# Neighbourhood attention: both heads' scores in one two-bank PSUM tile

## The chip, the cores and the metric

The kernel runs on one core of a Trainium2 chip. The metric is the device time of one execution in microseconds (us). Before the change the median of three runs is 2096.86 us (2092.8 to 2097.57).

## The reference, cut to what matters

The model has two layers over 512 latent tokens (a grid of 8 rows by 64 columns) and 256 context tokens. Each layer has one input projection whose columns go to three groups of heads: latent attention ("mla"), neighbourhood attention ("na") and a gated DeltaNet ("dn", a scan over chunks). The change is in the neighbourhood attention, which has 4 heads of width 64:

```
scale = NA_D ** -0.5
s_loc = einsum(qg, kb) * scale + bias        # each query: 8 rows x 16 columns around it
s_loc = where(col_ok, s_loc, -inf)
s_ctx = einsum(qg, ck) * scale               # and all 256 context keys
p = softmax(concatenate([s_loc, s_ctx], -1))
o = einsum(p_loc, vb) + einsum(p_ctx, cv)
```

In the first layer the 256 context tokens are queries too and read only context keys; in the second layer they are not.

## The kernel before, in words

Four heads are two pairs. The two heads of a pair lie in the two halves of the partitions (0 to 63 and 64 to 127), so that a product of one head uses 64 rows of TensorE. `attention()` goes over the pairs and, inside a pair, over blocks of 128 queries: six blocks in the first layer (four of latent tokens, two of context tokens), four in the second. That makes 12 blocks and 8 blocks.

For one block (lines 853 to 917 of the profile's numbering):

- The scores `s_na`. Each operand is held as a high and a low part, and three products (`nkh` with `nqh`, `nkl` with `nqh`, `nkh` with `nql`) are summed. A block of latent queries takes them over 256 local keys and again over 256 context keys: 12 products, 6 for each head. A block of context queries has 6, 3 for each head. The loops at 868 and 871 name the heads in turn, head 1 and then head 0.
- The softmax, head by head. VectorE (DVE) takes the maximum over the context scores (L877), adds the bias to the local scores and takes their maximum (L881), and makes the negated maximum (L883). ScalarE (ACT) takes the exponentials of the local part (L884) and, straight from PSUM, of the context part (L885): that is the last read of the scores. DVE then makes and applies the reciprocal (L889 to L891).
- TensorE transposes the weights (`tp_na`, L896), ACT copies one head's and DVE the other's to `pt` (L898), TensorE multiplies with the values (`o_na`), and ACT takes the result away (L909).

Before the change each head's scores are a PSUM tile of one bank, taken by `att_bank("s_na")` from a tag "S" with two buffers; the transposes and `o_na` share three more banks under the tag "T". A tile's buffer is free for the next block once all reads of the tile are done.

The order of the instructions on each engine isn't that of the source. A scheduler reorders the whole program when it is built, by its own reckoning of when operands and buffers are free, and each engine then runs its list strictly in order. `beside()` mixes steps of the DeltaNet scan (`ks`, `qs`, `yp`, `sp`, `oa`, and the chunk inverses `pp`, `yq`) and, in the first layer, columns of the modulation product (`acc_ada`, `tr_ada`) with the attention blocks. In the second layer, blocks of attention also stand between the last input projections (`acc_in`), by the string `TAIL`. After neighbourhood attention comes latent attention (`s_mla`, `tp_mla`, `o_mla`), mixed with the output projection `acc_o`.

All matrix products are issued by the helper at L104, so the profile tells them apart by tile name.

Of the kernel before, what the change touches and what calls it, by code (L numbers as in the profile page):

```python
# [9 lines left out]
F32 = mybir.dt.float32  # L10
# [7 lines left out]
P = 128  # L18
# [84 lines left out]
def mm(nc, out, lhsT, rhs, start=True, stop=True):  # L103
    nc.tensor.matmul(out, lhsT, rhs, start=start, stop=stop)  # L104
# [258 lines left out]
def layer(tc, nc, a, l, es_x, xT, env, nx):  # L363
    e = env
    V, S, G, PE = nc.vector, nc.scalar, nc.gpsimd, nc.tensor
# [467 lines left out]
    psA = pool(es_a, f"psA{l}", 1, PSUM, "left")  # L833
    att_n = BN

    def att_bank(name):
        tag = "S" if name[:2] == "s_" else "T"
        return psA.tile([P, 512], F32, tag=tag, name=name, bufs=att_n[tag])
# [8 lines left out]
    def attention():  # L847
        for pair in range(2):
# [4 lines left out]
            for qt in range(nT // P):  # L853
                is_ctx = qt >= 4
                tok = slice(qt * P, (qt + 1) * P)
                c0 = (0, 8, 24, 32, 0, 0)[qt]
                var = (0, 1, 1, 2, 0, 0)[qt]
                vb = ((0, 1), (6, 7), (7, 8), (2, 3), (), ())[qt] + (4, 5)
                lo_ = 256 if is_ctx else 0
                pts, ss = [], [att_bank("s_na") for j in range(2)]  # L860
                hs = [slice(64 * j, 64 * j + 64) for j in range(2)]
                cutk = lambda t, j: grid(t)[hs[j], :, c0:c0 + 32].rearrange("p r (b c) -> p b r c", b=2)


                trio = ((qh, kh), (qh, kl), (ql, kh))
                if not is_ctx:
                    for i, (q_, k_) in enumerate(trio):
                        for j in (1, 0):
                            mm(nc, ss[j][:, 0:256], q_[hs[j], tok], cutk(k_, j), i == 0, i == 2)
                for i, (q_, k_) in enumerate(trio):  # L870
                    for j in (1, 0):
                        mm(nc, ss[j][:, 256:512], q_[hs[j], tok], k_[hs[j], CTX], i == 0, i == 2)
                for j in range(2):
                    s_ = ss[j]
                    st_ = sn.tile([P, 8], F32, tag="st", name="st", bufs=4)
                    pr = sn.tile([P, 512], F32, tag="pr", name="pr", bufs=2)
                    V.reduce_max(out=st_[:, 0:1], in_=s_[:, 256:512], axis=AX.X)  # L877
                    if is_ctx:
                        V.tensor_scalar(out=st_[:, 2:3], in0=st_[:, 0:1], scalar1=-1.0, scalar2=None, op0=ALU.mult)
                    else:  # L880
                        V.tensor_tensor_reduce(out=pr[:, 0:256], in0=s_[:, 0:256], in1=gm[:, j, var].rearrange("p b r c -> p (b r c)"),  # L881
                                               scale=1.0, scalar=NEG, op0=ALU.add, op1=ALU.max, accum_out=st_[:, 1:2])
                        V.tensor_scalar(out=st_[:, 2:3], in0=st_[:, 0:1], scalar1=st_[:, 1:2], scalar2=-1.0, op0=ALU.max, op1=ALU.mult)  # L883
                        S.activation(out=pr[:, 0:256], in_=pr[:, 0:256], func=AF.Exp, bias=st_[:, 2:3], accum_out=st_[:, 3:4])  # L884
                    S.activation(out=pr[:, 256:512], in_=s_[:, 256:512], func=AF.Exp, bias=st_[:, 2:3], accum_out=st_[:, 4:5])  # L885
                    if is_ctx:
                        V.reciprocal(out=st_[:, 5:6], in_=st_[:, 4:5])
                    else:
                        tt(out=st_[:, 6:7], in0=st_[:, 3:4], in1=st_[:, 4:5], op=ALU.add)  # L889
                        V.reciprocal(out=st_[:, 5:6], in_=st_[:, 6:7])  # L890
                    V.tensor_scalar(out=pr[:, lo_:512], in0=pr[:, lo_:512], scalar1=st_[:, 5:6], scalar2=None, op0=ALU.mult)  # L891
                    tp = att_bank("tp_na")
                    nb = 2 if is_ctx else 4
                    for b in range(nb):
                        o2 = lo_ + b * P
                        PE.transpose(tp[:, b * P:(b + 1) * P], pr[:, o2:o2 + P], ident)  # L896
                    pt = sn.tile([P, 512], F32, tag="pt", name="pt", bufs=3)
                    (S.copy if j == 0 else V.tensor_copy)(out=pt[:, 0:nb * P], in_=tp[:, 0:nb * P])  # L898
                    pts.append(pt)
                o_ = att_bank("o_na")  # L900
                for b in range(len(vb)):
                    for j in (1, 0):
                        hd = 2 * pair + j
                        mm(nc, o_[j * 64:j * 64 + 64, 0:P], nav[:, vb[b], hd * 64:hd * 64 + 64], pts[j][:, b * P:(b + 1) * P],
                           b == 0, b == len(vb) - 1)
                if is_ctx:
                    S.copy(out=o_na[:, tok], in_=o_[:, 0:P])
                else:
                    S.copy(out=grid(o_na)[:, :, 16 * qt:16 * qt + 16], in_=o_[:, 0:P].rearrange("p (r c) -> p r c", c=16))  # L909
                if qt == nT // P - 1:  # L910
                    nc.sync.dma_start(out=d_o[2 + pair][:, 0:nT], in_=o_na[:, 0:nT])
                    if l == 0 and e.dbg is not None and "na" in e.dbg:
                        nc.sync.dma_start(out=e.dbg["na"][:, pair], in_=o_na)
                yield True

    na = attention()

    bm = C("bm32").rearrange("p (b c) -> p b c", b=4)
# [210 lines left out]
    psA, att_n, ada = pool(es_a, f"psM{l}", 1, PSUM, "left"), BM, iter(ADA[1])  # L1129
# [33 lines left out]
    for pair in range(2):  # L1163
# [30 lines left out]
        for qt in range(nT // P):  # L1194
# [5 lines left out]
            pts = []  # L1200
            for j in range(2):
# [4 lines left out]
                ss = []  # L1206
# [273 lines left out]
```

## Time and profile before

| | |
|---|---|
| median of the runs | 2096.86 us |
| the profiled execution | 2095.13 us, of which the span of instructions 2093.4 us |
| TensorE (PE) busy | 1939.7 us, 93% of the span |
| VectorE (DVE) busy | 1177.3 us, 56% |
| ScalarE (ACT) busy | 714.2 us, 34% |
| GpSimd (POOL) busy | 761.6 us, 36% |
| DMA | 232.55 MB, mean 111 GB/s |
| granted TensorE clock | 0.967 of full speed |

The span is dominated by the large products of the feed-forward part and the projections. Neighbourhood attention's scores run at 252 us (the first block, between the projections), from 353 to 450 us (the other eleven blocks of the first layer), and from 1412 to 1534 us (the eight blocks of the second layer). A share over the whole span says little about these stretches; the rows below are of the stretches.

### The profile page before, as it was taken

The numbers are of one execution on the slowest core, as the hardware profiler recorded it, in microseconds if no ns is written. First come the engines' busy times: TensorE is split into PE (matmuls) and PEld (weight loads), VectorE is DVE, ScalarE is ACT, GpSimd is POOL, SyncE is SP. The second block draws the span as 40 slices with busy tenths as digits, with TensorE's granted clock in tenths as the row PEclk, the third lists the DMA queues.
The fourth block names the chain that finished last, engine by engine and source line by source line (L and its number), as shares of the span: only waits on it lengthen the run. The fifth ranks groups of instructions, "written<-read, shape, count | busy, mean of one in ns | idle before, by whom it ended". The sixth has DMA issues, their size and how long they took to land. (4 is left out here: it accounts for less than half of the span.)

```text
span 2093.4 us, 32000 instructions
## 1 busy us (share of the span) xinstructions
PE 1939.7 (93%) x12746; PEld 1644.8 (79%) x12746; DVE 1177.3 (56%) x2045; ACT 714.2 (34%) x1385; POOL 761.6 (36%) x540
## 2 busy tenths in 40 slices
PE   6899998997998999999999988878998889999998
PEld 4778787876877888888888876767787678888887
DVE  4888914877467447256353358984678653213123
ACT  5343233334444121121122344233544443222234
POOL 3466133223323223222322443823322343444444
PEclk9999999998999999999999999999999899999999
DMA  7324253561212335245342431334332232333323
GB/s 283 84 74 140 97 165 110 187 197 59 91 59 85 127 121 161 89 126 156 103 131 76 130 79 61 114 124 129 100 98 70 78 96 71 101 91 95 103 92 93
DMA packets 119308, 232.55 MB, mean 111 GB/s; under 512 B 30516, under 2 KB 55988, under 8 KB 119032
## 3 DMA queue, kind: packets, MB, share of 16 engines
q1 hardware_dynamic: 119160, 230.51, 35.4%
q8 instruction: 100, 1.64, 0.3%
q14 instruction: 48, 0.39, 0.1%
HBM read 199.46 MB, written 31.01 MB: 110 GB/s over the span
## 5 line engine op out<-in xcount | busy, mean ns | idle before, releaser
L217 POOL TENSOR_TENSOR wl<-wr,wh 128x1024 fp32r<-128x1024 f32 (+2 forms) x188 | 440.6, 2344 | 846.1 <-ACT wh L216 826.4
L216 ACT CAST wh<-wr 128x1024 fp32r<-128x1024 f32 (+2 forms) x190 | 193.5, 1019 | 707.9 <-PE acc_gu L104 288.8
L104 PE MATMUL acc_gu<-fh,wh 128*128 128x512 f32 (+1 forms) x1024 | 358.5, 353 | 9.6 <-ACT fh L304 8.8
L104 PE MATMUL acc_gu<-fl,wh 128*128 128x512 f32 (+1 forms) x1024 | 359.8, 352 | 4.1 <-DVE fl L305 4.1
L104 PE MATMUL acc_gu<-fh,wl 128*128 128x512 f32 (+1 forms) x1024 | 358.8, 351 | 0.0
L104 PE MATMUL acc_in<-hh,wh 128*128 128x512 f32 (+1 forms) x640 | 228.3, 360 | 20.4 <-ACT xp L491 8.5
L104 PE MATMUL acc_in<-hl,wh 128*128 128x512 f32 (+1 forms) x640 | 227.7, 357 | 3.0 <-DVE hl L305 2.0
L1361 DVE TENSOR_TENSOR av<-acc_gu,av 128x768 f32<-128x768 f32 (+1 forms) x44 | 36.3, 824 | 337.8 <-PE acc_gu L104 330.9
L104 PE MATMUL acc_in<-hh,wl 128*128 128x512 f32 (+1 forms) x640 | 224.2, 355 | 2.0 <-POOL wl L217 2.0
L104 PEld LDWEIGHTS acc_gu<-fh,wh 128*128 128x128 f32 x1024 | 193.6, 190 | 37.3 <-ACT fh L304 11.0
L104 PEld LDWEIGHTS acc_gu<-fl,wh 128*128 128x128 f32 x1024 | 194.3, 190 | 30.4 <-DVE fl L305 4.3
L104 PEld LDWEIGHTS acc_gu<-fh,wl 128*128 128x128 f32 x1024 | 194.0, 190 | 26.1
L104 PEld LDWEIGHTS acc_in<-hh,wh 128*128 128x128 f32 x640 | 124.3, 195 | 46.1 <-ACT xp L491 10.2
L104 PE MATMUL acc_d<-al,wh 128*128 128x512 f32 (+1 forms) x444 | 157.2, 354 | 0.0
L104 PE MATMUL acc_d<-ah,wh 128*128 128x512 f32 (+1 forms) x444 | 157.2, 354 | 0.0
L104 PE MATMUL acc_d<-ah,wl 128*128 128x512 f32 (+1 forms) x444 | 156.1, 354 | 0.0
L254 DVE CUSTOM_DVE_ANT_0 junk<-wada,scb 128x1024 f32<-128x1024 f32 x112 | 146.2, 1305 | 5.9 <-DMA wada<-w_adaT 3.2
L104 PEld LDWEIGHTS acc_in<-hl,wh 128*128 128x128 f32 x640 | 125.2, 196 | 24.8 <-DVE hl L305 4.5
L104 PEld LDWEIGHTS acc_in<-hh,wl 128*128 128x128 f32 x640 | 124.1, 195 | 20.6 <-issue 3.1
L501 DVE SCALAR_TENSOR_TENSOR cy<-xp,cw,cy 128x770 f32<-128x770 f32 (+1 forms) x96 | 121.4, 1265 | 22.5 <-ACT cy L499 19.0
L1379 DVE SCALAR_TENSOR_TENSOR xT<-acc_d,mod,xT 128x512 f32<-128x512 f32 (+1 forms) x76 | 46.4, 634 | 155.3 <-PE acc_d L104 155.3
L1365 DVE TENSOR_TENSOR al<-av,ah 128x768 fp32r<-128x768 f32 (+1 forms) x44 | 100.4, 2282 | 35.2 <-ACT ah L1364 35.2
(390 smaller groups left out, 3777.2 us busy)
## 6 DMA issues: line engine op xcount, KB each, us to landing
wr<-w_gu SPq DMA_DIRECT2D x88, 512.0 KB, 3.5
wada<-w_adaT SPq DMA_DIRECT2D x56, 512.0 KB, 3.3
wr<-w_in SPq DMA_DIRECT2D x48, 512.0 KB, 3.5
wr<-w_dn SPq DMA_DIRECT2D x32, 448.0 KB, 3.3
wada<-w_ada SPq DMA_DIRECT2D x24, 512.0 KB, 3.5
wada<-w_ada SPq DMA_DIRECT2D x8, 1024.0 KB, 8.1
wr<-w_dn SPq DMA_DIRECT2D x16, 512.0 KB, 3.5
xT<-xT SPq DMA_DIRECT2D x16, 384.0 KB, 4.9
```

Of the source, the lines that this page charges most:

```text
L104: nc.tensor.matmul(out, lhsT, rhs, start=start, stop=stop)
L216: S.copy(out=hi[:, sl], in_=raw[:, sl])
L217: eng.tensor_tensor(out=lo[:, sl], in0=raw[:, sl], in1=hi[:, sl].bitcast(F32), op=ALU.subtract)
L254: V.tensor_tensor_reduce(out=junk, in0=w, in1=scb[:, s], scale=1.0, scalar=0.0, op0=ALU.mult, op1=ALU.add, accum_out=mod[l][:, part, j, s: ...
L501: stt(out=y[:, :wid], in0=xp[:, j:j + wid], scalar=w_(j), in1=y[:, :wid], op0=ALU.mult, op1=ALU.add)
L1361: tt(out=av[:, :nT], in0=accs[1][:, :nT], in1=av[:, :nT], op=ALU.mult)
L1365: after.append(tt(out=l_[:, :nT], in0=av[:, :nT], in1=h_[:, :nT].bitcast(F32), op=ALU.subtract))
L1379: stt(out=xT[:, m, st_], in0=acc, scalar=mod[l][:, 5, m, s:s + 1], in1=xT[:, m, st_], op0=ALU.mult, op1=ALU.add)
```

## The change

```diff
@@ -857,7 +857,8 @@
                 var = (0, 1, 1, 2, 0, 0)[qt]
                 vb = ((0, 1), (6, 7), (7, 8), (2, 3), (), ())[qt] + (4, 5)
                 lo_ = 256 if is_ctx else 0
-                pts, ss = [], [att_bank("s_na") for j in range(2)]
+                pts, s2 = [], psA.tile([P, 2, 512], F32, tag="S", name="s_na", bufs=1)
+                ss = [s2[:, j] for j in range(2)]
                 hs = [slice(64 * j, 64 * j + 64) for j in range(2)]
                 cutk = lambda t, j: grid(t)[hs[j], :, c0:c0 + 32].rearrange("p r (b c) -> p b r c", b=2)
```

The two heads' scores are now the two halves of one tile of two banks, with one buffer. The same two banks are used, each head still has its own, and no instruction is added or removed. What changes is that a block gets both banks at once, when all reads of the block before it are done. Lines after 860 have a number one higher in the changed kernel.

On TensorE, in the first layer, the second and third block's scores stood like this before (`s_na` scores, `ks` and `oa` products of the scan, `pp` of an inverse, `acc_ada` and `tr_ada` of the modulation):

```order
L104 MATMUL oa<-w,At 128x128 x4
L104 MATMUL pp<-p_3901,strips 32x32 x2
L104 MATMUL tr_ada<-cst,adarow 128x2
L104 MATMUL acc_ada<-wada,sc 32x128 x8
L104 MATMUL s_na<-nkh,nqh 128x256
L104 MATMUL s_na<-nkl,nqh 128x256
L104 MATMUL s_na<-nkh,nql 128x256
...
L104 MATMUL ks<-S_3168,dn_k 128x128 x4
L104 MATMUL pp<-p_3901,strips 32x32 x2
```

And in the changed kernel:

```order
L104 MATMUL o_na<-pt,nav 64x128 x8
L104 MATMUL acc_ada<-wada,sc 32x128 x8
L104 MATMUL ks<-S_3168,dn_k 128x128 x3
L104 MATMUL s_na<-nkh,nqh 128x256 x2
L104 MATMUL s_na<-nkl,nqh 128x256 x2
L104 MATMUL s_na<-nkh,nql 128x256 x2
...
L104 MATMUL ks<-S_3168,dn_k 128x128
L104 MATMUL qs<-S_3168,dn_q 128x128
L104 MATMUL tr_ada<-cst,adarow 128x2
```

Before, a stretch holds six products of one head, and the other head's six stand elsewhere; now "x2" is one product of each head, and the twelve stand together. All blocks of the changed kernel have this form.

On TensorE in the second layer, the second block stood between the projections of a weight tile before:

```order
L104 MATMUL acc_in<-hh_10575,wh 128x512
L104 MATMUL acc_in<-hl_10583,wh 128x512
L104 MATMUL s_na<-nkh,nqh 128x256
L104 MATMUL s_na<-nkl,nqh 128x256
L104 MATMUL s_na<-nkh,nql 128x256
...
L104 MATMUL acc_in<-hh_10575,wl 128x512
L104 MATMUL acc_in<-hh_10576,wh 128x512
```

In the changed kernel its first two products stand some 80 instructions further on, and the other ten some 170, behind the chunk inverse (`yq`) and the sum of squares for the latent queries (`ms_q`):

```order
L104 MATMUL yq<-strips,p_13093 32x32 x31
L104 MATMUL ms_q<-cst,sqs 128x2 x4
L104 MATMUL acc_in<-hh_10570,wh 128x512
L104 MATMUL acc_in<-hl_10578,wh 128x512
L104 MATMUL acc_in<-hh_10570,wl 128x512
L104 MATMUL s_na<-nkl,nqh 128x256 x2
L104 MATMUL s_na<-nkh,nql 128x256 x2
...
L104 MATMUL acc_in<-hh_10563,wh 128x512
```

The block has moved back in the row, so that more of other work stands between the first block's softmax and it.

On DVE in the first layer, the two heads' maxima of a block stood together before:

```order
L236 TENSOR_TENSOR mod_88<-tr_ada,bada 128x2
L231 COPY adarow<-acc_ada 128x128
L877 TENSOR_REDUCE st<-s_na 128x1 x2
L1055 TENSOR_TENSOR S_3591<-sp,S_3591 128x512
L1070 TENSOR_TENSOR o_3594<-oa,o_3594 128x512
L236 TENSOR_TENSOR mod_88<-tr_ada,bada 128x2
L881 ISA pr,st<-s_na,gmask_456 128x256
```

In the changed kernel one head's whole start goes first, and steps of the scan (`w`, `dn_q`) stand ahead of the other's:

```order
L878 TENSOR_REDUCE st<-s_na 128x1
L236 TENSOR_TENSOR mod_88<-tr_ada,bada 128x2
L882 ISA pr,st<-s_na,gmask_456 128x256
L882 ISA st 128x1
L899 COPY pt<-tp_na 128x512
L884 TENSOR_SCALAR st<-st 128x1
L1045 TENSOR_TENSOR w<-yp,scal 128x512
L1100 SCALAR_TENSOR_TENSOR dn_q<-o_tp,sml,z 128x4x128
L890 TENSOR_TENSOR st<-st 128x1
L878 TENSOR_REDUCE st<-s_na 128x1
```

Besides, the order of latent attention and of the output projection behind each neighbourhood attention is shuffled a little (in the first layer to about 560 us, in the second to about 1704 us); everything else is in the same order as before.

## Rows read from the trace of the kernel before

**Rows 1.** Windows: busy us of each engine, instructions, granted clock, DMA

```profile
core 0: us, PE busy (x) PEld busy (x) DVE busy (x) ACT busy (x) POOL busy (x), PEclk, DMA share, GB/s
350.00:450.00 100.00, 99.89 (x1386) 86.31 (x1386) 76.04 (x247) 36.28 (x129) 15.21 (x22) 0.98 0.56 172
450.00:560.00 110.00, 90.76 (x650) 76.15 (x650) 74.23 (x162) 50.66 (x147) 33.45 (x35) 0.91 0.34 110
1444.00:1453.00 9.00, 4.47 (x19) 3.08 (x18) 5.05 (x10) 7.30 (x14) 4.20 (x4) 0.80 0.93 211
1486.00:1536.00 50.00, 44.67 (x621) 37.50 (x620) 38.64 (x109) 21.51 (x66) 16.57 (x14) 0.90 0.36 112
1536.00:1640.00 104.00, 86.63 (x764) 74.14 (x759) 79.04 (x164) 47.12 (x143) 31.49 (x38) 0.95 0.25 73
```

**Rows 2.** Waits of PE from 343 to 455 us: total us, times, longest

```profile
PE tr_ada L104 <- DVE adarow L231: 1.6, 1, 1.6
PE sp L104 <- DVE w L1044: 1.0, 1, 1.0
```

**Rows 3.** Timeline of PE: start us, us, operation; one head alone

```profile
363.23 0.38 PE L104 MATMUL s_na<-nkh,nqh 64*128 64x256 f32 x1
363.45 0.28 PE L104 MATMUL s_na<-nkl,nqh 64*128 64x256 f32 x1
363.57 0.28 PE L104 MATMUL s_na<-nkh,nql 64*128 64x256 f32 x1
...
364.13 1.16 PE L104 MATMUL ks<-S,dn_k 128*128 128x128 f32 x8
...
380.71 0.38 PE L104 MATMUL s_na<-nkh,nqh 64*128 64x256 f32 x1
...
381.25 1.16 PE L104 MATMUL yp<-rr,Y 128*128 128x128 f32 x8
```

**Rows 4.** Timeline of PE: the first block, heads in turn

```profile
252.03 0.39 PE L104 MATMUL s_na<-nkh,nqh 64*128 64x256 f32 x2
252.25 0.28 PE L104 MATMUL s_na<-nkl,nqh 64*128 64x256 f32 x2
...
252.73 0.28 PE L104 MATMUL s_na<-nkh,nql 64*128 64x256 f32 x2
252.94 0.39 PE L104 MATMUL acc_v<-wh,hh 128*128 128x256 f32 x1
```

**Rows 5.** Windows of the tile s_na alone, columns of Rows 1 without POOL

```profile
235.00:300.00 65.00, 0.98 (x12) 0.78 (x12) 0.00 (x0) 0.00 (x0) 0.97 0.45 128
345.00:550.00 205.00, 17.74 (x108) 13.44 (x108) 14.05 (x36) 13.01 (x48) 0.94 0.46 145
1340.00:1550.00 210.00, 12.90 (x96) 9.98 (x96) 12.27 (x32) 8.79 (x32) 0.93 0.38 116
```

**Rows 6.** Timeline of PE, second layer: the second block

```profile
1447.96 0.39 PE L104 MATMUL s_na<-nkh,nqh 64*128 64x256 f32 x1 [0.22 <-ACT pr L885]
...
1450.82 0.58 PE L104 MATMUL s_na<-nkh,nqh 64*128 64x256 f32 x1 [1.87 <-ACT pr L885]
```

**Rows 7.** Waits of PE from 1486 to 1536 us

```profile
PE tp_na L896 <- DVE pr L891: 2.7, 2, 1.4
PE o_na L104 <- DVE pt L898: 1.5, 1, 1.5
PE s_na L104 <- ACT pr L885: 0.6, 2, 0.4
```

**Rows 8.** Timeline of DVE: one block's softmax begins, first layer

```profile
364.24 0.76 DVE L877 TENSOR_REDUCE st<-s_na 128x1 f32<-128x256 f32 x2 [0.58 <-PE s_na L104]
```

**Rows 9.** Timeline of ACT: the same block's last read of the scores

```profile
370.93 0.46 ACT L885 ACTIVATE pr<-s_na,st 128x256 f32<-128x256 f32 x1
```

**Rows 10.** Waits of PE from 455 to 560 us, the longest

```profile
PE yp L104 <- DVE rr L1039: 5.9, 2, 4.9
```

## The prediction

> **What bounds the kernel now.** I first asked the windows view for the stretches in which the scores run, since shares over the whole span mix them with the big products. In the first layer, from 350 to 450 us, PE is busy 99.9 of 100 us and DVE 76 [rows 1]. The list of PE's waits over this stretch has two entries, 2.6 us together, and the scores are in neither [rows 2]. So PE sets the pace there, and a microsecond of PE work taken away is a microsecond, as long as DVE keeps up. In the second layer, from 1486 to 1536 us, PE is busy 44.7 of 50 us and DVE 38.6 [rows 1], and PE's waits are for DVE (`pr`, `pt`) and, with 0.6 us, for the exponentials that free the scores' bank [rows 7]. There PE and DVE share the bound. Behind both stretches comes latent attention, where PE is idle for 19 of 110 us and 17 of 104 us, by 90.76 and 86.63 us busy [rows 1], in the first layer mostly on the scan's `rr` from DVE [rows 10].
>
> **What a pair costs, alone and in turn.** The timeline shows a stretch of six products of one head from 363.23 us to the next work at 364.13: 0.90 us; products follow each other every 0.12 us, and the stretch pays about 0.2 us for its first step and its last [rows 3]. A stretch of three (a context block's head) takes from 380.71 to 381.25: 0.54 us [rows 3]. The first block, in which both heads' products happen to alternate, takes from 252.03 to 252.94: 0.91 us for twelve [rows 4]. So two products that use different halves of the rows run beside each other, and a block whose heads go in turn costs what one head costs alone.
>
> **The sum.** Nothing is removed or added; 216 products are put in another order. Of the tile's busy time in the first layer, 17.74 us for 108 products [rows 5], a part overlaps the next work: the six of rows 3 would end 0.28 us after their last start, the twelve of rows 4 are busy 0.98 us [rows 5] but hold PE for 0.91. Taking 0.07 us off each of the 21 stretches that the timeline has there leaves 16.3 us. Afterwards the eleven blocks cost 7 x 0.91 + 4 x 0.54 = 8.5 us, the context blocks' 0.54 being an estimate (three pairs at 0.12 and the 0.2 of a stretch). That takes 7.8 us off PE. In the second layer 12.90 us of busy time [rows 5] in 12 stretches is 12.1 us by the same step; afterwards eight blocks at 0.91 us, and 0.2 us each for two that the new order still cuts in two, are 7.7 us: 4.4 us less. It is less than in the first layer because several blocks there go in turn already. Third, one block of the second layer stands too early before: PE is idle for 1.87 us, until 1450.82, for an exponential of the block before [rows 6]. The new order puts this block behind other work, so that the wait has a reason to go. Together 14.1 us at most.
>
> What of it arrives? In the first layer the stretch is PE's own, and DVE's 76 us of work fit in the 92 that would be left. But the scan's DVE steps are then crowded, and the wait for `rr` of up to 4.9 us behind the stretch [rows 10] has less work ahead of it; for that I take 1.5 us off: 6.3 us arrive. In the second layer half of PE's idle time is set by DVE already [rows 7], so I take half of 4.4 us, 2.2. Of the 1.87 us, half: the projections beside it stood still for a weight as well (PE is busy 4.5 of the 9 us around, DMA at 93% [rows 1]), and what is freed may be waited for there. 6.3 + 2.2 + 0.9 = 9.4 us. From the profiled execution's 2095.13 us that leads to 2085.7; the median of the runs is 1.7 us higher, so 2087.4, rounded to 2087.5.
>
> **What the change adds.** One wait: a block's first product now waits until both heads of the block before have had their exponentials, where it waited for one. Behind it on PE stand steps of the scan and the transposes `tp_na` of the block before, which in turn feed DVE and ACT. The trace has no tile of two banks, so I bound this from both sides. At the good end it costs nothing: in the block of rows 8 and 9 DVE begins at 364.24 us and the last exponential ends at about 371.4, 7.2 us, and that with the scan's work in between; eleven blocks in 100 us are one per 9 us, and the new order puts scores roughly a period apart. At the bad end each of the 18 blocks that follow another in their layer waits as the block of rows 6 did, 1.87 us: 34 us. The rows from 343 to 455 us have no such wait at all [rows 2], those from 1486 to 1536 two, with 0.6 us [rows 7]; I take zero for the first layer, and the halving above covers the second.
>
> **Rivals.**
>
> *DVE takes over.* Both heads' scores are now ready in the same moment, while DVE works on one head after the other, in the new order with steps of the scan before the second. If DVE's latency rather than PE sets the period, PE's 7.8 and 4.4 us turn into waits of `tp_na` and `o_na` for DVE, and the time stays at 2094 to 2100 us. For it: the waits of rows 7, and DVE at 77% in both stretches [rows 1]. Against it: in the first layer PE waits for DVE only 2.6 us in 112 [rows 2]. The Trainium skill, page "TensorEngine Tiling (Array Packing)", section "PSUM Bottleneck", speaks for this rival: it says that packing the array speeds TensorE but not the emptying of PSUM, which may then become the bottleneck. In the trace the second layer agrees in part (2.7 + 1.5 us of waits for DVE in 50 us), the first doesn't. I give it 0.21.
>
> *The pair's wait becomes the period.* One tile, one buffer: if scores, both softmaxes and the release take longer than PE's work for a block, every block waits. Break-even is at 12 us over 18 blocks, 0.67 us a block; from 1.0 us on the kernel is slower by more than can be told from nothing. At 1.87 us a block [rows 6] it is 34 - 12 = 22 us slower, some 2119. For it: the 7.2 us from the first maximum to the last exponential [rows 8, 9], plus 0.9 for the scores, is close to a period of 8.4 us (92 us for eleven blocks). Against it: those 7.2 us contain waiting in DVE's queue, and the row's own steps are 0.76 us for both maxima and 0.46 for an exponential. I give it 0.11.
>
> *The shuffled order behind it is better too.* The stretches of latent attention are reordered as well, and hold 19 and 17 us of idle PE [rows 1]. If a quarter of it goes, and the 14.1 us arrive nearly whole, the time is some 2076 to 2080. The same shuffle could as well cost as much, which would fall in the first rival's place. 0.18.
>
> *The heads' products don't run beside each other after all* I leave without a chance of its own: rows 4 show it done.
>
> **How the numbers follow.** A difference of under 0.3% (6.3 us) can't be told from none here; faster is thus below 2090.6. The forecast (2082 to 2093) has 0.50, of which 0.43 lie below 2090.6; the better order has 0.18, DVE's rival 0.21, the pair's wait 0.11. Faster 0.43 + 0.18 = 0.61, the same 0.07 + 0.21 = 0.28, slower 0.11. The range leaves out the pair's wait and the better order's lower half: 2077 to 2100; the forecast's own is 2082 to 2093.
>
> **What would show it.** In the profile after: every block's scores in one stretch of 0.91 us (0.54 for context blocks), the tile's busy time down from 0.98 + 17.74 + 12.90 = 31.6 us [rows 5] to about 18 (16 blocks at 0.98 us and four at 0.6); the eleven blocks done by about 442 us instead of 450; the wait of 1.87 us gone. Against me would be waits of `s_na` for `pr` (L886 then) of about a microsecond in each block, which is the pair's wait, or longer waits of `tp_na` and `o_na` for `pr` and `pt`, which is DVE's rival. If the stretches shrink as said and the end doesn't come earlier, the gain went into latent attention's waits for DVE.

## The result and the profile after

The changed kernel takes 2077.15 us (median of 4 runs, 2074.75 to 2078.46) against 2097.22 us for the kernel before in the same series (2092.8 to 2097.91): a ratio of 0.9902, 95% interval 0.9889 to 0.9914. That is 20.1 us less; forecast were 9.4. The profiled execution took 2074.75 us, its span is 2073.0 us.

**Where the time went.** A total over the span would hide it, so the table takes the starts of the same PE instructions in both traces and gives the distance between them by stage (us). The first instruction of a stage ends the one before; "up to 335 us" is left out of the sum, because it differs from execution to execution without a change in order. Each row comes from one execution of each kernel; where two kernels have the same order, rows of one execution each differ by up to about 2 us.

| stage, from its first instruction to the next | before | after | difference |
|---|---|---|---|
| first layer, scan and neighbourhood attention (335 to 474 us before) | 139.0 | 132.1 | -6.9 |
| first layer, latent attention and output projection | 173.8 | 169.7 | -4.1 |
| feed-forward and first input projections | 615.7 | 615.8 | +0.1 |
| second layer, convolutions, gates, last input projections (to 1411 us before) | 147.6 | 144.5 | -3.1 |
| second layer, neighbourhood attention (to 1558 us before) | 146.9 | 139.7 | -7.2 |
| second layer, latent attention and output projection | 161.7 | 161.5 | -0.2 |
| feed-forward to the end | 374.0 | 374.1 | +0.1 |

The sum is 21.3 us, of which the start of this one execution gave 0.9 back. Forecast were 6.3 us in the first layer's neighbourhood attention and 3.1 us in the second's; 4.1 and 3.1 us came from stages in which I had expected nothing. One boundary isn't quite the same work: in the changed kernel all twelve scores of the second layer's first block stand ahead of the product at which the second layer's neighbourhood attention begins here, before they stand behind it. They take 1.25 us there (1394.60 to 1395.85 us), so on equal work the gate row is about 4.3 us and the row of the second neighbourhood attention about 5.9 us.

**What the scores look like now.** The timeline of PE, second block of the first layer, columns as in [rows 3]:

```profile
362.43 0.39 PE L104 MATMUL s_na<-nkh,nqh 64*128 64x256 f32 x2
362.66 0.28 PE L104 MATMUL s_na<-nkl,nqh 64*128 64x256 f32 x2
...
363.14 0.28 PE L104 MATMUL s_na<-nkh,nql 64*128 64x256 f32 x2
363.35 0.49 PE L104 MATMUL ks<-S,dn_k 128*128 128x128 f32 x2
```

Each row is one product of each head, and the block holds PE from 362.43 to 363.35 us: 0.92 us for twelve, where [rows 3] had 0.90 us for six. The tile's own windows answer [rows 5]:

```profile
235.00:300.00 65.00, 0.98 (x12) 0.78 (x12) 0.00 (x0) 0.00 (x0) 0.97 0.45 127
345.00:550.00 205.00, 9.37 (x108) 7.10 (x108) 14.92 (x38) 13.30 (x48) 0.94 0.46 148
1340.00:1550.00 210.00, 8.72 (x96) 6.57 (x96) 12.15 (x32) 8.82 (x32) 0.97 0.39 117
```

PE is busy with the scores for 0.98 + 9.37 + 8.72 = 19.1 us instead of 31.6; "about 18" was said. By the time from each score's start to the start of what follows it, summed (called "held by scores" below), the first layer's stretch went from 16.3 to 8.6 us, where the prediction had 16.3 and 8.5. The last score there starts 91.3 us after the first instead of 96.4; the prediction had the blocks done by 442 us, and it is 446, since the first of them also starts 2.0 us later (355.1 instead of 353.1) and part of the saving shows only behind the last score.

**The stretches.** The windows view over the same bounds as [rows 1] (the second layer's work now lies some 15 to 20 us earlier in them):

```profile
350.00:450.00 100.00, 97.50 (x1449) 85.32 (x1450) 83.28 (x266) 40.66 (x144) 19.84 (x29) 0.98 0.60 189
450.00:560.00 110.00, 90.96 (x628) 75.34 (x628) 72.68 (x158) 50.68 (x140) 35.55 (x33) 0.92 0.31 98
1486.00:1536.00 50.00, 45.48 (x772) 39.55 (x764) 40.37 (x104) 22.92 (x67) 11.32 (x12) 0.99 0.35 100
1536.00:1640.00 104.00, 86.60 (x633) 72.72 (x635) 82.33 (x179) 48.61 (x151) 26.64 (x35) 0.95 0.25 74
```

In the first layer PE is still the engine without slack, 97.5 of 100 us, and DVE has gone from 76 to 83: it does more of its work in the same time and still keeps up. In the second layer, 1486 to 1536 us, the granted clock is 0.99 where it was 0.90 [rows 1]; I had read past that column, and it comes back below. The waits of PE in the two stretches that answer [rows 2] and [rows 7], 343 to 447 us and 1465 to 1516 us:

```profile
PE tr_ada L104 <- DVE adarow L231: 1.6, 2, 1.1
PE sp L104 <- DVE w L1045: 1.5, 2, 1.4
PE o_na L104 <- ACT Y L985: 0.7, 1, 0.7
...
PE yp L104 <- DMA vp<-d_v: 2.3, 1, 2.3
PE yp L104 <- DVE rr L1040: 1.5, 1, 1.5
PE tp_na L897 <- DVE st L890: 1.1, 1, 1.1
PE o_na L104 <- DVE st L884: 1.0, 1, 1.0
```

No score waits for an exponential `pr` any more, in either layer: the one tile with one buffer has added no such wait, and the 1.87 us of [rows 6] are gone. Of the 5.9 us that `yp` waited for `rr` behind the first layer's stretch [rows 10], 2.8 are left.

**What I had not seen.** The section on the change says that outside the attention stretches everything stands in the same order as before. That is wrong. In the second layer the scheduler has also moved steps of the convolutions and gates, on every engine, from about 1290 us on, well ahead of the first score there. One place of it stands out; the timeline of the kernel before, three engines:

```profile
1366.87 0.22 DVE L678 TENSOR_TENSOR tmp<-R,Bk 96x62 f32<-96x62 f32 x1 [6.53 <-ACT Bk L669]
1367.01 1.01 DVE L501 SCALAR_TENSOR_TENSOR cy<-xp,cw,cy 128x770 f32<-128x770 f32 x1
...
1370.83 1.00 DVE L501 SCALAR_TENSOR_TENSOR cy<-xp,cw,cy 128x770 f32<-128x770 f32 x1
...
1371.86 0.85 ACT L503 ACTIVATE th<-cy 128x770 f32<-128x770 f32 x1 [4.14 <-DVE cy L501]
1372.62 0.57 ACT L491 COPY xp<-acc_in 128x512 f32<-128x512 f32 x1
...
1373.23 0.79 PE L104 MATMUL acc_in<-hh,wh 128*128 128x512 f32 x1 [6.66 <-ACT xp L491]
```

Read it from below. PE waits 6.66 us for `xp`, the copy that empties a projection's bank. `xp` stands on ACT behind `th`, which waits for the convolution's last step `cy` on DVE. Two such steps stand on DVE behind `tmp`, the first step of the chunk inverse, and `tmp` waits 6.53 us for `Bk`, which ACT makes when a DMA has landed. The steps themselves had nothing to wait for, as an experiment below shows. In the changed kernel:

```profile
1354.72 1.01 DVE L501 SCALAR_TENSOR_TENSOR cy<-xp,cw,cy 128x770 f32<-128x770 f32 x1
1355.78 0.22 DVE L678 TENSOR_TENSOR tmp<-R,Bk 96x62 f32<-96x62 f32 x1
...
1356.54 0.85 ACT L503 ACTIVATE th<-cy 128x770 f32<-128x770 f32 x1
1357.28 0.58 ACT L491 COPY xp<-acc_in 128x512 f32<-128x512 f32 x1
...
1357.91 0.50 PE L104 MATMUL acc_in<-hh,wh 128*128 128x512 f32 x1 [1.88 <-ACT xp L491]
```

The last `cy` stands ahead of `tmp`, and PE waits 1.88 us instead of 6.66. No score has a part in this.

### The profile page after: what moved, and what is told of

Same layout as the page of the kernel before. It is cut to its first block, busy times and chain, and to the rows that moved or that the text cites. A ratio compares the mean times of both kernels' runs of the same rounds, so it can differ in the third digit from the quotient of the medians.

```text
span 2073.0 us, 31991 instructions
## 1 busy us (share of the span) xinstructions
PE 1917.8 (93%) x12746; PEld 1625.3 (78%) x12746; DVE 1172.4 (57%) x2045; ACT 714.4 (34%) x1385; POOL 758.7 (37%) x540
## 4 chain that ended last, share of the span: by engine, by line
PE 70%; DVE 15%; ACT 4%; DMA 3%; issue 3%; POOL 3%; SPq 1%; DVEq 0%; POOLq 0%; ACTq 0%
PE acc_gu L104 29%; PE acc_d L104 15%; PE acc_in L104 9%; PE acc_o L104 4%; DVE cy L501 3%; PE acc_v L104 1%; DVE tmp L678 1%; PE s_mla L104 1%; PE o_mla L104 1%; PE acc_ada L104 1%; ACT pr L1219 1%; PE yp L104 1%; DVE R L680 1%; PE sp L104 1%; PE s_na L104 1%
## 5 line engine op out<-in xcount | busy, mean ns | idle before, releaser
L501 DVE SCALAR_TENSOR_TENSOR cy<-xp,cw,cy 128x770 f32<-128x770 f32 (+1 forms) x96 | 116.1, 1209 | 21.3 <-ACT cy L499 19.3
```

Of the source, the lines that this page charges most:

```text
L501: stt(out=y[:, :wid], in0=xp[:, j:j + wid], scalar=w_(j), in1=y[:, :wid], op0=ALU.mult, op1=ALU.add)
```

## The experiments

Twelve kernels ran, in three series, each beside the kernel before (medians 2098.1, 2097.06 and 2096.41 us). The first four change the source and leave the order to the scheduler. Since the scheduler then also shuffles the rest, the other eight are the kernel before (each head its own tile) with the order of every engine written out. Their diff is the same but for the list `ISSUE` (left out here): each instruction gets an edge to its forerunner on its engine, which orders the two and adds no semaphore. Before's own order written out was not run by itself. The changed kernel's was, and takes the same time as the changed kernel (below), so the edges alone cost nothing that shows there. Medians and stage lengths carry noise: differences of medians are given with the range of the interval where it matters.

```diff
         emit(tc, aps, out)
+        pin_order(tc, nc)
...
+    for engine, steps in json.loads(zlib.decompress(base64.b85decode(ISSUE))).items():
+        at, prev = 0, None
+        for step in steps:
+            at += step
+            ins = traced[engine][at]
+            if prev is not None:
+                tc.add_manual_dep(ins, prev.name, mybir.DependencyInfo(mybir.DependencyClass.NoSync, mybir.DependencyReason.DATA), reason="pin")
+            prev = ins
```

### The heads apart again

In the changed kernel the products of a block are taken head by head; the place of the block and the order of all else stay.

```diff
-                for i, (q_, k_) in enumerate(trio):
-                    for j in (1, 0):
-                        mm(nc, ss[j][:, 256:512], q_[hs[j], tok], k_[hs[j], CTX], i == 0, i == 2)
...
+                jobs += [(j, i, slice(256, 512), q_, k_[hs[j], CTX]) for i, (q_, k_) in enumerate(trio) for j in (1, 0)]
+                jobs.sort(key=lambda t: -t[0])
+                prev = None
+                for j, i, cs, q_, rhs in jobs:
+                    with tc.issue_after(prev.ins) if prev is not None else ExitStack():
+                        prev = PE.matmul(ss[j][:, cs], lhsT=q_[hs[j], tok], rhs=rhs, start=i == 0, stop=i == 2)
```

> The changed kernel, but inside each block's stretch of scores all products of head 1 go first and then all of head 0. Every other instruction of every engine stands where it stands in the changed kernel; the one tile of two banks and its wait stay. Theory A (the gain is the two heads' products running beside each other): a block of 12 costs 12 x 0.12 + 0.19 = 1.63 us in place of 0.91 and a context block 0.91 in place of 0.54, so 16 x 0.72 + 4 x 0.36 = 13 us of PE work come back and the time is about 2088 to 2091. Theory B (the gain is the order into which the scheduler put everything else): the time stays within 3 us of the changed kernel, 2075 to 2080. In between, by how much PE was the bound: each us of the 13 that doesn't show was hidden.

Measured: 2087.48 us, ratio to before 0.994 (0.992 to 0.9959): by the medians 10.6 us faster than before and 10.3 slower than the changed kernel (by the ratios 8.0). So in the changed kernel's order going in turn is worth 8 to 10 us, some four tenths to half of the change. That is next to the 2088 to 2091 us expected if going in turn were all of the gain, and yet 10.6 us of gain are left without it. But the price isn't the one that I had worked out. The timeline of PE, the same block:

```profile
362.46 0.38 PE L875 MATMUL s_na<-nkh,nqh 64*128 64x256 f32 x1
362.68 0.28 PE L875 MATMUL s_na<-nkl,nqh 64*128 64x256 f32 x1
362.80 0.28 PE L875 MATMUL s_na<-nkh,nql 64*128 64x256 f32 x1
362.80 0.39 PE L875 MATMUL s_na<-nkh,nqh 64*128 64x256 f32 x2
...
363.51 0.28 PE L875 MATMUL s_na<-nkh,nql 64*128 64x256 f32 x1
363.71 0.49 PE L104 MATMUL ks<-S,dn_k 128*128 128x128 f32 x2
```

Twelve products, head 1's six queued ahead of head 0's, take 1.25 us, not the 1.63 us expected: rows of two products in the middle show that head 0's first three start beside head 1's last three, which stand ahead of them in PE's list. In the first layer PE is held by scores for 11.0 us against 8.6 in turn, and its stage is only 2.3 us longer than in the changed kernel (134.4 against 132.1 us). The second layer's neighbourhood attention is 4.3 us longer (144.0 against 139.7), its latent attention 3.5 (165.0 against 161.5). These stages overstate it: this profiled execution is 3.1 us above its kernel's median and the changed kernel's 2.4 us below, so the two spans differ by 15.9 us where the medians differ by 10.3.

### The two-bank tile in one layer only

```diff
-                pts, ss = [], [att_bank("s_na") for j in range(2)]
+                pts = []
+                if l == 0:   # the other kernel: l == 1
+                    s2 = psA.tile([P, 2, 512], F32, tag="S", name="s_na", bufs=1)
+                    ss = [s2[:, j] for j in range(2)]
+                else:
+                    ss = [att_bank("s_na") for j in range(2)]
```

First layer only:

> The two-bank tile in the first layer alone. The first layer is in the order of the changed kernel, and so is the second layer's gate and projection stretch (about 1290 to 1400 us), which the scheduler reordered as well though no score stands in it; from the second layer's neighbourhood attention on, the scores are in two tiles again. The trace of the changed kernel gained 10 us in the first layer, 5 in the gate stretch and 5 to 6 behind it. Theory A (only scores in turn bring anything, the gate stretch's 5 us differ by chance from execution to execution): about 2087. Theory B (the order of the gate stretch brings its 5 us each time): about 2082, with the gate stretch as short as in the changed kernel.

Second layer only:

> The two-bank tile in the second layer alone. First layer and the second layer's gate stretch are in the order of the kernel before, the second layer's attention in that of the changed kernel nearly throughout. Theory A (scores in turn, 4.4 us of PE work, and the wait of 1.87 us gone): 2091 to 2094. Theory B (the order behind the gate stretch brings 5 to 6 us with latent attention's part of 4): about 2091 to 2092, and the gate stretch stays as long as before with its wait of several us for the convolution's input. If it is faster than 2088, the gate stretch's gain is not due to its order.

Measured: first layer only 2072.64 us, ratio 0.9874 (0.9855 to 0.9894), by the medians 4.5 us faster than the changed kernel, though the two intervals overlap a little; second layer only 2092.42 us, ratio 0.9968 (0.9957 to 0.9979). The first is the surprise. Its second layer has two tiles and the heads apart (in the stage of neighbourhood attention, which holds seven of the eight blocks, the scores hold PE for 11.0 us, 6.8 in the changed kernel), and yet it is no longer. That stage takes 139.3 us against 139.7, but here 16 products of the scan (`ks`, `qs`) have moved out of it into latent attention. From the convolutions to the output projection every kernel has the same instructions; these three rows together take 441.9 us here, 445.7 in the changed kernel and 456.1 before. So the second layer can be as fast without the pairing, in another order of the scheduler's.

### Two tiles, the products tied in turn

The tiles are those of before; against the kernel before only the ties of the first experiment are new, without the sorting by head, so that the heads go in turn.

```diff
...
+                jobs += [(j, i, slice(256, 512), q_, k_[hs[j], CTX]) for i, (q_, k_) in enumerate(trio) for j in (1, 0)]
+                prev = None
+                for j, i, cs, q_, rhs in jobs:
+                    with tc.issue_after(prev.ins) if prev is not None else ExitStack():
+                        prev = PE.matmul(ss[j][:, cs], lhsT=q_[hs[j], tok], rhs=rhs, start=i == 0, stop=i == 2)
```

> The kernel before with its two tiles of one bank, and the products of a block tied to each other so that the heads must go in turn (an ordering edge from each product to the next, no semaphore). The gate stretch keeps the order of before. In most blocks one product stands alone ahead and eleven follow in turn: 0.31 + 0.85 us a block in place of 0.91. Theory A (in turn is what counts): some 8 to 10 us faster than before, 2087 to 2089, without the two-bank tile. Theory B (the tile's one release, and the order it leads to, is what counts): no faster than 2093.

Measured: 2089.31 us, ratio 0.9959 (0.9943 to 0.9975). By stages it says little of the pairing: 3.0 us came from the first layer's neighbourhood attention, 2.7 from the second's, 5.4 from the second's latent attention, whose order the scheduler had also made anew. This run made me write the order out for what followed.

### The changed kernel's order with two tiles

The list of every engine is that of the changed kernel; the tiles are those of before.

> The kernel before, with its two one-bank tiles, but with every engine's instructions pinned by ordering edges to the order of the changed kernel. Only the wait differs from the changed kernel: each head's products wait for their own bank alone. If the tile's one release costs time in its own right (the pair's wait of the prediction), this is faster than the changed kernel, by 1 us a block up to 18 us, 2060 to 2074. If it costs nothing and the whole effect of the new tile is the order it leads the scheduler to, it is the same: 2075 to 2079.

Measured: 2078.81 us, ratio 0.9914 (0.9901 to 0.9928), which the interval doesn't tell from the changed kernel's 0.9902. The pair's single release and its wait cost nothing that can be measured, and the tile gives nothing by itself: the change is the order that it leads to, the pairing included.

### Before's order, each block's products brought together in turn

Only PE's list differs from before's: the products of a block stand together at the place of the later head.

> The kernel before in its own order, pinned on every engine, with one edit: each block's products of both heads are brought together on PE, heads in turn, at the place where the later head's first product stood. All other engines keep the order of before. Theory A (what counts is that the pairs run beside each other): 7.8 us in the first layer arrive, 2 to 4 in the second, and 2085 to 2089 results. Theory B (the gain is mostly the reordering of everything else): at most 5 us, 2092 or more, since DVE and ACT keep their old order and now get the earlier head later.

Measured: 2086.71 us, ratio 0.9951 (0.9938 to 0.9965), 10.3 us less, with 7.3 to 13.0 in the interval. This is the pairing that the prediction worked out, done alone. By stages the gain is mostly the first layer's: neighbourhood attention from 139.0 to 131.9 us; the second layer's took 146.9 us, as before, though its scores shrank from 12.1 to 10.1 us of PE. The second layer's three rows together are 2.8 us shorter, but 2.0 us shorter too in the kernel with the first layer alone in the new order (below), whose second layer has neither the pairing nor a new order; so by these traces some 0.8 us of that at most can be laid to the pairing. The wait of [rows 6] isn't gone here, it is 2.46 us: the block stays where it was.

### One part in the changed kernel's order, the rest in before's

The gate stretch (about 1290 to 1420 us):

> The kernel before, pinned to its own order, except that the gate and projection stretch of the second layer (about 1290 to 1420 us, in which no score but the first block's end stands) is in the order of the changed kernel. No score is moved in the first layer. If that order is what made the changed kernel 4.6 us shorter there (in two kernels with that order it was 4.5 and 4.6, in one 3, in three with the old order 0), this is 4 to 5 us faster than before: 2092 to 2094. If it was something the earlier arrival brought (DMA, clock), it is within 2 us of before.

Measured: 2091.17 us, ratio 0.9974 (0.9963 to 0.9984), 5.9 us less, with 3.4 to 7.8 in the interval. The only scores that move are those of the second layer's first block, which go ahead by some products.

The first layer:

> The kernel before, pinned, with the first layer alone in the order of the changed kernel (scores in turn, and the scan, modulation and latent attention shuffled with them), and from the feed-forward part on the order of before. Two one-bank tiles. From the traces: 10 to 11 us faster, 2086 to 2088. Theory A says 7.8 us of that are the scores; together with p2 the rest shows what the shuffle of the other instructions is worth (3 us by the trace of the changed kernel).

Measured: 2088.88 us, ratio 0.9959 (0.9946 to 0.9973), 8.2 us less, with 5.7 to 11.3 in the interval, where 10 to 11 were expected. It holds the first layer's pairing and the new order around it, and isn't faster than the pairing in before's order (10.3). So by whole times the first layer's new order adds nothing that can be told.

Both:

> The kernel before, with the first layer's attention and the gate stretch in the changed kernel's order, and the second layer from the scores on in the order of before, its heads apart. If the parts add up, 8.2 + 5.9 = 14.1 us less, some 2083, and the last 6 us of the change are the second layer's attention, where the forecast had 3.1. If the first layer and the gates carry all of it together: 2077.

Measured: 2082.37 us, ratio 0.9933 (0.992 to 0.9945), 14.0 us less (11.5 to 16.8) against the 14.1 of the sum. The parts add up within this noise, and the 6 us that are left of the change's 20.1 are the second layer from the scores on, order and pairing together.

### Two steps of a convolution ahead of the waiting one

Before's order, but on DVE the two steps `cy` behind the waiting `tmp` stand ahead of it. Then the same with the blocks brought together.

> The kernel before, every engine in its own order, but on DVE in the second layer the last two steps of one convolution (`cy`, L501) stand ahead of the first `tmp` of the chunk inverse (L678) instead of behind it; nothing else moves, and no score does. In the trace of before DVE stands 6.53 us at that `tmp`, which waits for ACT's copy `Bk`; behind it are the two steps, behind these ACT's `th` and `xp` (L503, L491), and PE waits 6.66 us for `xp`. Theory: this is where the change won in the gate stretch, since its order has one of the two steps ahead of the `tmp` and PE then waits 1.88 us. With both ahead, `th` can begin when ACT is through with `Bk` and the cast behind it (1367.7 us instead of 1371.9), so 4.2 us less: some 2093. Rival: the gate stretch's gain comes from the many other steps that stand otherwise there; then 2097, as before, and PE waits elsewhere.

> The kernel before in its own order, with each block's products brought together in turn (which alone gave 10.3 us) and, besides, the two steps of the convolution ahead of the `tmp` on DVE. If the pairing and the wait in the gate stretch are separate causes they add up: 10.3 + 4.2 = 14.5 us, some 2082.5. If both took the same idle time the sum is smaller, 2086.

Measured: the two steps alone 2093.79 us, ratio 0.9988 (0.9979 to 0.9996): 2.6 us less, with 0.8 to 4.4 in the interval, where 4.2 were expected. The timeline of this kernel:

```profile
1361.55 3.12 DVE L501 SCALAR_TENSOR_TENSOR cy<-xp,cw,cy 128x770 f32<-128x770 f32 x3
1368.93 0.22 DVE L678 TENSOR_TENSOR tmp<-R,Bk 96x62 f32<-96x62 f32 x1 [4.26 <-ACT Bk L669]
...
1371.05 0.50 PE L104 MATMUL acc_in<-hh,wh 128*128 128x512 f32 x1 [2.25 <-ACT xp L491]
```

DVE still waits 4.26 us for `Bk`, but nothing that PE needs stands behind it, and PE waits 2.25 us instead of 6.66. So two moved steps take 4.4 us off this wait; a microsecond of it is waited for again at the sum of squares `ssq` (3.7 us, 2.7 before). It is one shown cause of the gate stretch's gain, not all of its 5.9 us. Together with the pairing: 2082.6 us, ratio 0.9937 (0.992 to 0.9953), 13.8 us less. 10.3 and 2.6 add up to 12.9, which fits separate causes; the interval, 9.9 to 16.8 us, would also hold 10.3 alone, so it doesn't prove them.

### The fastest order, with the second layer in turn

> The order of the kernel with the two-bank tile in the first layer only, the fastest so far at 2072.6 us, and in the second layer each block's twelve products in turn instead of one head after the other; each head has its own tile. The tile's starts there should fall from 11.0 us to some 7.3. If PE sets the pace there, 3.7 us less: 2069. If DVE does, as half of the forecast's second layer assumed, 0 to 2 us less: 2071 to 2073.

Measured: 2072.7 us, ratio 0.9884 (0.9871 to 0.9897), the same as without the pairing in the second layer (0.9874, 0.9855 to 0.9894). The scores of the seven blocks hold PE for 8.4 us instead of 11.0; 7.3 were expected. The windows of the second layer's neighbourhood attention, between the same two instructions, columns as in [rows 1]; first without the pairing there:

```profile
1397.70:1536.90 139.20, 125.14 (x1436) 106.59 (x1436) 87.53 (x217) 62.42 (x147) 45.25 (x30) 0.97 0.38 112
```

and with it:

```profile
1400.60:1540.70 140.10, 122.61 (x1436) 104.36 (x1436) 88.15 (x217) 62.39 (x147) 45.24 (x30) 0.96 0.38 111
```

PE has 2.5 us less to do and the stage is no shorter: the idle time grew by 3.4 us. The waits of PE from 1400 to 1540 us show where, without the pairing and with it:

```profile
PE sp L104 <- DVE w L1049: 3.3, 1, 3.3
PE s_na L104 <- ACT pr L890: 2.0, 3, 1.3
PE acc_in L104 <- ACT wh L216: 1.9, 1, 1.9
```

```profile
PE sp L104 <- DVE w L1044: 3.7, 1, 3.7
PE s_na L104 <- ACT pr L885: 3.4, 4, 2.3
PE acc_in L104 <- ACT wh L216: 2.6, 1, 2.6
```

The scores wait longer for the exponentials, and the projections for their weight. One block shows how, without the pairing and with it:

```profile
1435.79 0.58 PE L104 MATMUL s_na<-nkh,nqh 64*128 64x256 f32 x1 [1.32 <-ACT pr L890]
1439.43 0.58 PE L104 MATMUL s_na<-nkh,nqh 64*128 64x256 f32 x1 [2.27 <-ACT pr L885]
```

With the heads apart head 1's six products run while head 0's bank isn't free yet. In turn five of them stand behind head 0's first product, and PE waits 2.27 us instead of 1.32. That is what the prediction's second rival said of a pair, in a block that the order leaves too early; in the changed kernel the block has moved back, and the wait isn't there.

## Why the prediction was half right

**The direction and the mechanism held.** Two products on different halves of the rows run beside each other, a block in turn costs 0.92 us (0.91 forecast), and the tile's busy time is 19.1 us. Brought about alone, in before's order, this is worth 10.3 us (2086.71); the sum had 9.4. That these agree so well is partly luck: 3.1 us of the sum were the second layer's, where the pairing alone gave some 0.8 at most by its trace, and about 3 us of the 10.3 came from rows in which the sum has nothing.

**The first layer's 6.3 us: right.** The stage lost 6.9 us in the changed kernel and 7.1 with the pairing alone. The 1.5 us that I took off for the wait for `rr` were hardly needed: with the pairing alone that wait grew from 5.9 to 6.5 us, and in the changed kernel it is 2.8.

**The second layer's 2.2 us: wrong as a mechanism; the 0.9: right in its reason.** With the pairing alone the second layer's neighbourhood attention stayed at 146.9 us, and in the fastest order it gained nothing either. Only inside the changed kernel's order does it count, by the first experiment's single execution 4.3 us. I had halved PE's saving because DVE sets half of the idle time [rows 7]; in two of three orders none of the saving arrived. Of the third term, the wait of 1.87 us is gone where the order moves the block back, and stays (2.46 us) where it doesn't.

**The step that failed is "What arrives?"** It added up the scores and took the order of everything else as neutral, with its gain behind the scores as a rival of 0.18. The order was about half of the result: 20.1 us in all, 10.3 by the pairing alone. It shows in three places where the sum has nothing or too little:

- The gate stretch, 3.1 us by the table (4.3 on equal work) and 5.9 us (3.4 to 7.8) by the kernel that moves it alone. In one kernel with the same order there, the heads apart again, its row is 146.9 us, hardly shorter than before, at a clock of 0.93. I had gone through the difference in order from the first layer's scores on and from the second layer's, and had not looked at what lies ahead of the second. The wait of 6.66 us was in the trace of before.
- The second layer's neighbourhood attention, 7.2 us by the table and 5.9 on equal work, where 3.1 were forecast. Neither part makes it alone. The pairing in before's order left the row at 146.9 us; the changed kernel's order with the heads apart has 144.0, without the first block's scores, and the whole change 139.7. With the tile in the second layer alone, which has both and the same work in the row as before, it is 140.2. In the order of the kernel with the tile in the first layer only, the pairing isn't needed. What the order does there is read from the traces and wasn't tried by itself. In the kernel before, PE's clock falls to its lower level twice within the stage. The first fall comes behind a wait for a weight and inside the wait of [rows 6], the second behind a wait of 1.46 us for `pt`; two waits of `tp_na` for `pr` [rows 7] then lie inside the second spell and are not what began it:

```profile
1447.01 0.50 PE L104 MATMUL acc_in<-hh,wh 128*128 128x512 f32 x1 [2.43 <-ACT wh L216]
...
1503.51 1.09 PE L896 MATMUL tp_na<-cst,pr 128*128 128x128 f32 x4 [1.26 <-DVE pr L891]
```

  The windows view of before (its first row belongs to the wait of 6.66 us in the gate stretch):

```profile
1372.00:1376.00 4.00, 2.77 (x11) 2.58 (x11) 3.93 (x11) 2.88 (x5) 0.07 (x2) 0.50 0.76 253
1449.40:1456.10 6.70, 5.29 (x15) 4.29 (x16) 5.58 (x16) 3.03 (x7) 4.39 (x4) 0.50 0.82 234
1498.00:1500.50 2.50, 2.22 (x15) 1.84 (x16) 2.37 (x7) 0.94 (x5) 2.50 (x2) 1.00 1.00 347
1500.60:1510.80 10.20, 7.54 (x90) 6.15 (x91) 9.21 (x22) 3.16 (x10) 5.56 (x5) 0.50 0.33 117
1410.90:1557.70 146.80, 132.26 (x1464) 112.08 (x1463) 88.67 (x220) 62.60 (x147) 46.03 (x30) 0.94 0.38 109
```

  and of the changed kernel, the first row behind the wait of 1.88 us, the last again the whole stage:

```profile
1357.00:1361.00 4.00, 2.58 (x18) 2.32 (x19) 4.00 (x6) 1.73 (x5) 2.20 (x4) 1.00 0.25 96
1432.60:1439.30 6.70, 3.98 (x10) 3.14 (x10) 5.34 (x9) 3.74 (x8) 6.26 (x4) 0.50 1.02 244
1483.80:1487.10 3.30, 3.30 (x73) 3.01 (x74) 2.28 (x9) 0.31 (x1) 3.30 (x3) 0.50 0.81 274
1397.70:1537.40 139.70, 125.21 (x1454) 106.07 (x1452) 87.80 (x217) 62.89 (x147) 44.94 (x29) 0.96 0.40 115
```

  PE is busy 7.0 us less over the stage, 1.25 of it the first block's scores. The other seven blocks' scores hold it for 4.2 us less (11.0 before, 6.8 after). A granted clock of 0.50 is the 1.2 GHz level; the first spell at it is as long as before, 6.7 us, and the second 3.3 us instead of 10.2. Length times the missing share of the clock is 146.8 x 0.06 = 8.8 us before and 139.7 x 0.04 = 5.6 us after, an estimate of what the clock cost at most. With before's order in the second layer and all else as changed the clock is 0.91 and the row 147.1 us. But the kernel with the two moved steps has 0.95 and 147.0, so the clock isn't all of it. How much is the clock, how much the scores and how much the waits themselves stays open.
- The first layer's latent attention, 4.1 us. Part of it is order: the seven traces with the changed order there have 169.4 to 171.8 us, the five with before's 172.4 to 173.8, 2.7 us apart on the mean. But two of the seven (171.7 and 171.8) have a clock of 0.92 and the other five, the changed kernel's among them, 0.94 or 0.95; so some 2 us of the 4.1 go with the clock of the single execution, and by whole times nothing of it could be told. Which wait it is I didn't follow up.

**The rivals.** "The pair's wait becomes the period" (0.11) fell: the same order with two tiles takes the same time, and no score waits for `pr`. It shows in single blocks where the pairing comes without the new order (2.46 and 2.27 us). "DVE takes over" (0.21) fell for the first layer and for the total. In the second layer PE's saving did turn into waits in the fastest order, where 2.5 us less of PE's work gave nothing; but the waits that grew most there are for ACT (`pr` by 1.4 us, `wh` by 0.7), so that DVE sets the pace there isn't shown. The rule of the Trainium skill, page "TensorEngine Tiling (Array Packing)", section "PSUM Bottleneck", that packing doesn't speed the emptying of PSUM, agrees with that stage (`s_na` waits 3.4 us for `pr` instead of 2.0) and not with the first layer's. "The shuffled order behind it is better too" (0.18, 2076 to 2080) is where the time lies, though for other reasons than it gave: idle PE in the two latent attentions went from 24.5 to 23.3 us and from 22.8 to 27.2, so no quarter of it went, and the gate stretch's gain lies ahead of the attention, not behind it.

**What may be faster still.** The two-bank tile in the first layer alone takes 2072.64 us, 0.9874 (0.9855 to 0.9894) of before; the changed kernel's 0.9902 (0.9889 to 0.9914) just overlaps that. What it has over the changed kernel lies where only the second layer's order, tile and pairing differ: by the traces the spans differ by 3.4 us, and the second layer's neighbourhood and latent attention together by 3.6 (297.5 us instead of 301.2). Since neither the tile nor, in that order, the pairing changes the time, what is left is the order.

## What to carry to other kernels

When a scheduler orders the whole program, one changed tile is two changes, the local one and a new draw of the order behind it and, here, of a stretch ahead of it; compare the order of every engine from the first instruction to the last before forecasting, and check in the trace of before which long waits the new order happens to pass. To price the local edit, write the old order out and change only that; here it gave 10.3 us for the pairing, and 2.6 us for two steps of 1 us moved past a waiting one. When lengths of stages are compared, count that both sides hold the same instructions. Here DVE's wait of 6.53 us for `Bk` held up work for which PE then waited 6.66 us, so look for the work queued behind a wait whose consumer is the busiest engine.

## What the runs showed of the hardware

- Products of two heads on different halves of the rows overlap even when one head's six are queued ahead of the other's: 1.25 us for twelve, against 0.92 in turn and 0.90 for six of one head followed by work on all rows [rows 3]. Head 0's first product starts at 362.80 us beside head 1's third, and head 1's last three, which stand ahead of it in the list, start after it. Twice 0.90 is the price where other work stands between the heads, as in [rows 3].
- After an interruption PE can run at half speed for a while: the first product behind the 6.66 us wait took 0.79 us, that behind the 1.88 us wait 0.50, and around it the granted clock of the kernel before was 0.50 (1372 to 1376 us) where the changed kernel's was 1.00 (1357 to 1361 us). A wait of PE can thus cost more than its own length.
